# One in-order queue for loads and stores, and tiles of twice the size, in a streaming gated-GELU kernel

## The chip, the cores and the metric

The kernel runs on one core of one Trainium2 chip. The metric is the time of the program on the device in microseconds (us), as the median of several runs. The profiled span is about 1.9 us shorter than that time (474.1 against 476.0 us before). Most differences here are below 2%, so each run was timed beside the kernel before, on the same chip in the same rounds.

## The reference

The input is `x`, 32 x 512 x 2048 float32 (134.2 MB). The last axis is split in two halves; the output is 32 x 512 x 1024 float32 (67.1 MB):

```python
x1, x2 = x[..., :1024], x[..., 1024:]
gelu_x1 = 0.5 * x1 * (1 + erf(x1 / np.sqrt(2)))
return (gelu_x1 * x2).astype(np.float32)
```

Every byte is read or written once, 201.3 MB in all. There is no reuse.

## The kernel before

Rows are laid out so that each of the 128 partitions holds R consecutive rows of a tile. With R = 4 a load moves 4 MB, 32 KB contiguous per partition, and a store 2 MB, 16 KB per partition. There are 32 tiles. Loads are issued by SP (`nc.sync`), stores by ACT (`nc.scalar`): two queues.

```python
    R = 4
    x_t = x_flat.rearrange("(n p r) d -> n p r d", p=P, r=R)
    o_t = out_flat.rearrange("(n p r) d -> n p r d", p=P, r=R)
    n_tiles = x_t.shape[0]

    xpool = ctx.enter_context(tc.tile_pool(name="xpool", bufs=4))
    opool = ctx.enter_context(tc.tile_pool(name="opool", bufs=4))

    for i in range(n_tiles):
        x_tile = xpool.tile([P, R, dim], x.dtype)
        nc.sync.dma_start(out=x_tile, in_=x_t[i])

        o_tile = opool.tile([P, R, half], out.dtype)
        for r in range(R):
            nc.scalar.activation(out=x_tile[:, r, :half], in_=x_tile[:, r, :half],
                                 func=mybir.ActivationFunctionType.Gelu)
            nc.vector.tensor_mul(out=o_tile[:, r, :], in0=x_tile[:, r, :half],
                                 in1=x_tile[:, r, half:])
        nc.scalar.dma_start(out=o_t[i], in_=o_tile)
    # ... (launch code cut)
```

## Time and profile before

| | before |
|---|---|
| time, median | 476.0 us (475.94 to 476.09) |
| profiled span | 474.1 us |
| DMA queues' packet time | 98.9% of 16 engines' span |
| DVE, ACT busy | 31%, 27% |

From the page of the kernel before, parts 1 to 3. In part 2 the span is cut into 40 slices; a DMA digit of 9 means that the 16 DMA engines were at least 90% busy in that slice. In part 3, q1 carries SP's loads and q10 ACT's stores.

```profile
DVE 148.2 (31%) x128; ACT 125.9 (27%) x129; POOL 0.2 (0%) x4
...
DMA  8999999999999999999999999999999999999995
...
q1 hardware_dynamic: 4608, 134.22, 65.8%
q10 hardware_dynamic: 4608, 67.11, 33.1%
```

So the DMA engines bound the kernel, and only the first and the last slice have room. The next view cuts the end of the span into short windows. The columns are window, its length, busy time of DVE, ACT and POOL, the TensorE clock, then the DMA share and GB/s; the first line is one tile's period from the middle.

```profile
60.00:74.54 14.54, 4.63 (x4) 3.90 (x4) 0.00 (x0) 1.00 1.00 433
...
460.00:462.00 2.00, 0.55 (x1) 1.64 (x2) 0.00 (x0) 1.00 1.07 459
462.00:464.00 2.00, 2.00 (x3) 2.00 (x3) 0.00 (x0) 1.00 0.71 303
464.00:466.00 2.00, 2.00 (x2) 0.25 (x1) 0.00 (x0) 1.00 0.04 16
466.00:467.00 1.00, 0.08 (x1) 0.00 (x0) 0.00 (x0) 1.00 0.27 115
467.00:470.00 3.00, 0.00 (x0) 0.00 (x0) 0.00 (x0) 1.00 0.95 396
470.00:472.00 2.00, 0.00 (x0) 0.00 (x0) 0.00 (x0) 1.00 0.93 393
```

A share of 1.00 in the middle: nothing to win there but cheaper packets. (A share can pass 1, by 0.07 in these lines, because a packet's whole time is booked where it starts.) Between 462 and 467 us there is a hole: all earlier transfers have drained, and the last store waits for the last tile's arithmetic.

The trace also has a record for every DMA packet: start, duration, bytes and queue, but not the engine. Two things can be worked out from these records. First, a 32 KB load packet takes 1213 ns and a 16 KB store packet 611 ns at the median (27 bytes per ns and engine). Second, every load and store here ends with 16 4-byte packets (1024 for the 64 of them), by continuity one on each engine; the time from the first to the last of these 16 tells how far the engines stand apart. I call it the *spread*. (Which packets belong to one engine can be told by continuity: on an engine, a packet starts about 4 ns before the record of the one before it ends.)

### The profile page before, as it was taken

How to read it: one execution, taken by the hardware profiler on the slowest of the kernel's cores; microseconds unless marked ns; L12 is line 12 of the kernel's file. 1: busy time of each engine (PE TensorE's matmuls, PEld its weight loads, DVE VectorE, ACT ScalarE, POOL GpSimd, SP SyncE). 2: the span in 40 equal slices, each digit the busy share in tenths (PEclk: the TensorE clock that was granted, in tenths of full speed). 3: DMA queues.
4: the chain of work that ended last, by engine and by line, in shares of the span. 5: the costliest groups of instructions: out<-in, count | busy, mean ns of one | idle time of the engine just before them, and what ended most of it. 6: DMA issues, size and time to landing. Idle time of an engine off the chain costs nothing.

```text
span 474.1 us, 509 instructions
## 1 busy us (share of the span) xinstructions
DVE 148.2 (31%) x128; ACT 125.9 (27%) x129; POOL 0.2 (0%) x4
## 2 busy tenths in 40 slices
DVE  0333321333312333123332133331233321333213
ACT  1423331133321333213333123332133331233311
POOL 0000000000000000000000000000000000000000
DMA  8999999999999999999999999999999999999995
GB/s 354 406 456 408 455 417 445 419 444 420 442 420 443 421 440 427 435 433 430 438 427 452 412 451 413 452 413 452 413 451 420 445 419 444 421 440 423 440 423 225
DMA packets 9220, 201.36 MB, mean 425 GB/s; under 512 B 1024, under 2 KB 1024, under 8 KB 1024
## 3 DMA queue, kind: packets, MB, share of 16 engines
q1 hardware_dynamic: 4608, 134.22, 65.8%
q10 hardware_dynamic: 4608, 67.11, 33.1%
q14 instruction: 4, 0.03, 0.0%
HBM read 134.22 MB, written 67.11 MB: 425 GB/s over the span
## 4 chain that ended last, share of the span: by engine, by line
another core or an unknown queue 48%; DVE 27%; DMA 13%; ACT 7%; issue 2%; ACTq 2%; DVEq 0%
DVE o_tile L45 27%; DMA x_tile<-in_x_dram 13%; ACT x_tile L40 7%; ACTq L50 2%; DVEq L76 0%; ACTq L40 0%
## 5 line engine op out<-in xcount | busy, mean ns | idle before, releaser
L45 DVE TENSOR_TENSOR o_tile<-x_tile 128x1024 f32<-128x1024 f32 x128 | 148.2, 1219 | 317.9 <-ACT x_tile L40 317.9
L40 ACT ACTIVATE x_tile<-x_tile 128x1024 f32<-128x1024 f32 x128 | 124.7, 1044 | 337.6 <-DMA x_tile<-in_x_dram 337.6
L40 ACT ACT_TABLE_LOAD x1 | 1.3, 1283 | 0.7 <-PEq L65 0.7
L65 POOL MEMSET const-uint8-127<- 128x1 uint8 x1 | 0.1, 102 | 0.0
L65 POOL MEMSET const-bfloat16-1.0<- 128x1 bf16 x1 | 0.1, 101 | 0.0
L65 POOL MEMSET const-float32-0.0<- 128x1 f32 x1 | 0.1, 99 | 0.2 <-issue 0.2
L65 POOL MEMSET const-float32-1.0<- 128x1 f32 x1 | 0.1, 99 | 0.0
## 6 DMA issues: line engine op xcount, KB each, us to landing
x_tile<-in_x_dram SPq DMA_DIRECT2D x32, 4096.0 KB, 52.3
out_dram<-o_tile ACTq DMA_DIRECT2D x32, 2048.0 KB, 23.4
```

Of the source, the lines that this page charges most:

```text
L40: nc.scalar.activation(out=x_tile[:, r, :half], in_=x_tile[:, r, :half], func=mybir.ActivationFunctionType.Gelu,)
L45: nc.vector.tensor_mul(out=o_tile[:, r, :], in0=x_tile[:, r, :half], in1=x_tile[:, r, half:],)
L50: nc.scalar.dma_start(out=o_t[i], in_=o_tile)
L65: nc = _bacc.Bacc("TRN2", target_bir_lowering=False, num_devices=1)
```

## The change

The intent: one queue in a fixed order instead of two that compete; half as many, twice as large transfers; and a shorter tail, because the last tile's store is cut in four. The diff's core (launch code and renamings cut):

```diff
-    R = 4
+    R = 8
...
-    xpool = ctx.enter_context(tc.tile_pool(name="xpool", bufs=4))
-    opool = ctx.enter_context(tc.tile_pool(name="opool", bufs=4))
+    xpool = ctx.enter_context(tc.tile_pool(name="xpool", bufs=2))
+    opool = ctx.enter_context(tc.tile_pool(name="opool", bufs=2))
+    def load(i):
+        x_tile = xpool.tile([P, R, dim], x.dtype, name="x_tile")
+        nc.sync.dma_start(out=x_tile, in_=x_t[i])
+        return x_tile
+
+    ahead = [load(0), load(1)]
     for i in range(n_tiles):
-        x_tile = xpool.tile([P, R, dim], x.dtype)
-        nc.sync.dma_start(out=x_tile, in_=x_t[i])
+        x_tile = ahead.pop(0)
+        o_tile = opool.tile([P, R, half], out.dtype, name="o_tile")
...
+        pieces = 1 if i < n_tiles - 1 else 4
+        step = R // pieces
+        for k in range(pieces):
+            for r in range(k * step, (k + 1) * step):
+                ...   # Gelu and multiply of row r, as before
+            rows = slice(k * step, (k + 1) * step)
+            nc.sync.dma_start(out=o_t[i][:, rows, :], in_=o_tile[:, rows, :])
+        if i + 2 < n_tiles:
+            ahead.append(load(i + 2))
-        nc.scalar.dma_start(out=o_t[i], in_=o_tile)
```

The queue of SP becomes L0 L1 S0 L2 S1 L3 ... L15 S14 and four pieces of S15.

More of the change, by code (lines that the diff above doesn't have):

```diff
@@ L7 @@
 from concourse._compat import with_exitstack
+GELU = mybir.ActivationFunctionType.Gelu
 @with_exitstack
@@ L29 @@
     n_tiles = x_t.shape[0]
-    xpool = ctx.enter_context(tc.tile_pool(name="xpool", bufs=4))
-    opool = ctx.enter_context(tc.tile_pool(name="opool", bufs=4))
-    for i in range(n_tiles):
-        x_tile = xpool.tile([P, R, dim], x.dtype)
-        nc.sync.dma_start(out=x_tile, in_=x_t[i])
-        o_tile = opool.tile([P, R, half], out.dtype)
-        for r in range(R):
-            nc.scalar.activation(
-                out=x_tile[:, r, :half],
-                in_=x_tile[:, r, :half],
-                func=mybir.ActivationFunctionType.Gelu,
-            )
-            nc.vector.tensor_mul(
-                out=o_tile[:, r, :],
-                in0=x_tile[:, r, :half],
-                in1=x_tile[:, r, half:],
-            )
-        nc.scalar.dma_start(out=o_t[i], in_=o_tile)
+    xpool = ctx.enter_context(tc.tile_pool(name="xpool", bufs=2))
[5 more added lines that the diff above has]
+    ahead = [load(0), load(1)]
+    for i in range(n_tiles):
+        x_tile = ahead.pop(0)
[4 more added lines that the diff above has]
+            for r in range(k * step, (k + 1) * step):
+                nc.scalar.activation(
+                    out=x_tile[:, r, :half], in_=x_tile[:, r, :half], func=GELU
+                )
+                nc.vector.tensor_mul(
+                    out=o_tile[:, r, :],
+                    in0=x_tile[:, r, :half],
+                    in1=x_tile[:, r, half:],
+                )
+            rows = slice(k * step, (k + 1) * step)
+            nc.sync.dma_start(out=o_t[i][:, rows, :], in_=o_tile[:, rows, :])
+        if i + 2 < n_tiles:
+            ahead.append(load(i + 2))
 _INS = ['x']
```

## The prediction

> **What bounds the kernel now.** The 16 DMA engines. The page's DMA row is 9 tenths or more in every slice but the first and last; the two queues take 65.8% + 33.1% = 98.9% of 16 engines' span. ACT is busy 27%, DVE 31%. Cut into stretches of 14.54 us (one tile's period) from 60 to 452 us, each shows DMA share 1.00 to 1.01 and 432 to 433 GB/s. In the packet records a 32 KB load packet takes 1213 ns at the median, a 16 KB store packet 611 ns, whether loads run alone (5 to 18 us), both interleave, or stores run alone (460 to 463 us). With 256 of each per engine that is 310.5 + 156.4 = 466.9 us of a span of 474.1. The other 7 us are the start (about 1.5), the drain after the last store (about 2) and a hole at the end: the DMA share is 0.71 in 462 to 464 us, 0.04 in 464 to 466, 0.27 in 466 to 467. Store 30 has drained, and the last tile's Gelu and multiply (460.4 to 466.1) must end before its store starts. The hole is 0.58 + 1.92 + 0.73 = 3.2 us.
>
> **What the change does.**
> 1. Stores move from ACT's queue to SP's. [...] the load queue alone already has share 1.0. Worth 0. ACT loses 32 issues of 0.36 us, off the critical path.
> 2. In-order waits: the queue becomes L0 L1 S0 L2 S1 L3 ... Store i and load i+2 both wait for tile i's multiply, so neither holds up the other. Compute of an 8-row tile is an estimated 1.1 + 8 x 1.22 = 11 us after its load; the queue then still holds about 18 us of work (store i-1 9.7, load i+1 19.4), in the first round 8 us. The engines never run dry.
> 3. Packets double. 1213 - 2 x 611 = -9 ns: about 9 ns are fixed per packet. Halving 512 packets per engine saves an estimated 2.3 us; the 8 KB packets of the last stores give 0.2 back. Worth 2 us, or 1 if 64 KB rows are cut in two.
> 4. The tail. Store 14 stands behind load 15 and lasts 9.7 us while the last tile computes; its first quarter is ready after 3.6 us, its last after 11. So the 3.2 us hole goes.
>
> **Sum.** 474.1 - 3.2 - 2.0 = 468.9 us of span; times are 1.9 us above the span: **471.0 us**, 8 in 10 between **469.0 and 473.5**, about 1% faster. Chances: faster by over 2% 0.02 (466.5 us is less than data plus start and drain), within 2% 0.94, slower by over 2% 0.04.
>
> **Right if:** the DMA row stays at 9 until 2 us before the end, share 1.00 in every period of about 29 us, no hole after the last load; load packets near 2417 ns, store packets near 1213; SP waits for DVE only.
>
> **Wrong if:** one queue has a bubble at a store's end. [...] load-to-load boundaries in the first 20 us show no loss, but no store-to-load boundary within one queue is in this trace. At 0.5 us each they would cost 8 us and eat the gain. Or 64 KB packets behave differently, or one engine lags.

## The result, and the profile after

| | before | after |
|---|---|---|
| time, median of 4 runs | 475.97 us | 475.73 us |
| lowest to highest | 475.91 to 476.09 | 474.72 to 476.17 |
| profiled span | 474.1 us | 472.7 us (of the 474.72 us run) |

The ratio is 0.9993, 95% interval 0.9978 to 1.0007. Ratios are the mean time of one kernel's fast runs over that of the other's in the same rounds, so not quite the ratio of the medians. The predicted 471.0 us (469.0 to 473.5) was too low: nearly nothing was gained. The runs after differ by 1.5 us, those before by 0.2 us.

From the page after, parts 1 to 3:

```profile
DVE 146.8 (31%) x128; ACT 124.2 (26%) x129; POOL 0.2 (0%) x4
...
DMA  8999999999999999999999999999999999999996
...
q1 hardware_dynamic: 5040, 201.33, 99.0%
```

SP's waits after (who waited for whom, us in total, times, longest):

```profile
SPq L58 <- DVE o_tile L52: 447.1, 19, 31.3
SPq L86 <- DMA out_dram<-o_tile: 8.7, 1, 8.7
```

And windows after, one 8-row period from the middle, then the end:

```profile
70.00:99.08 29.08, 9.17 (x8) 7.68 (x8) 0.00 (x0) 1.00 1.00 433
...
456.00:460.00 4.00, 4.00 (x4) 4.00 (x5) 0.00 (x0) 1.00 0.89 381
460.00:464.00 4.00, 2.60 (x3) 0.03 (x1) 0.00 (x0) 1.00 0.99 418
464.00:467.00 3.00, 0.00 (x0) 0.00 (x0) 0.00 (x0) 1.00 1.01 429
467.00:468.00 1.00, 0.00 (x0) 0.00 (x0) 0.00 (x0) 1.00 0.99 418
468.00:470.00 2.00, 0.00 (x0) 0.00 (x0) 0.00 (x0) 1.00 0.39 164
470.00:472.00 2.00, 0.00 (x0) 0.00 (x0) 0.00 (x0) 1.00 0.10 41
```

Most of the prediction is visible: SP waits for DVE alone until its final wait, the DMA share is 1.00 in the middle, and the hole before the last store is gone. But the span does not end at 468 us plus the drain. In 468 to 472 us the share is 0.39 and then 0.10: most of the 16 engines have finished, and a few still work. The packet records say the same. Sorted, the ends of the 16 engines' last packets are (us from the span's start):

```
before: 471.89 471.89 471.89 471.89 471.91 471.92 471.92 471.94 471.96 471.97 471.98 471.98 471.99 472.02 472.02 472.83
after:  467.93 468.02 468.04 468.05 468.05 468.20 468.45 468.57 468.75 468.83 468.90 469.98 470.59 470.67 471.06 471.41
```

(These are ends of 4-byte packets, one for each engine, put together by continuity. The last 16 such packets of the trace would not do after the change: the slowest engines are more than one piece, 2.5 us, behind, so four of the 16 would be ends of the piece before.) The earliest engines finish where the prediction wanted all of them. Where does the difference come from? The spread at the end of successive DMAs shows it (start of the 16 packets: spread, both in us):

```
before, loads : 21.9: 0.44   138.6: 0.49   167.7: 1.18   313.2: 1.18   458.6: 1.24
after, L0..L3 : L0 21.7: 0.64   L1 42.1: 0.67   S0 51.7: 0.67   L2 71.1: 0.73   S1 80.8: 0.73   L3 100.1: 0.89   S2 109.8: 0.89
after, later  : L4 129.1: 1.15  S3 138.8: 1.15  L5 158.2: 1.39  S4 167.8: 1.39  L6 187.2: 1.70  ...  L15 448.4: 3.48
```

After the change the spread grows from load to load and never from a load's end to the next store's end. It is the last packet of a load, the one in front of a store, that is stretched. A 64 KB load packet normally takes 2418 ns; the 16 last packets of L1 (at 39 us, in front of S0) took 3240 to 3868 ns, 1.07 us more in the mean. At later boundaries some engines lose 0 to 0.6 us and others nothing. No engine of the core computes at 39 us (tile 0 is done at 32.9, tile 1 starts at 43.1 us), so it is not traffic of ACT or DVE. Before, load packets after the first 4 us lose only 0.58 us per engine in all, 0.51 of it when the first store joins the loads at about 21 us; one engine lags by another 0.7 us from 153 us on, and then almost nothing changes. I call it *stretch*.

**Theory A.** In one in-order queue every load-to-store boundary is a turn of the engine; turns stretch the last load packet, differently on each engine, nothing brings the engines together again, and the program ends with its slowest engine. **Rival B.** The 64 KB packets or the large tiles do it.

### The profile page after: what moved, and what is told of

Its sections match the earlier page's. It is cut to its first block, busy times and chain, and to the rows that moved or that the text cites. A ratio compares the mean times of both kernels' runs of the same rounds, so it can differ in the third digit from the quotient of the medians.

```text
span 472.7 us, 394 instructions
## 1 busy us (share of the span) xinstructions
DVE 146.8 (31%) x128; ACT 124.2 (26%) x129; POOL 0.2 (0%) x4
## 4 chain that ended last, share of the span: by engine, by line
DMA 79%; DVE 15%; ACT 2%; SPq 1%; issue 0%; DVEq 0%; ACTq 0%
DMA x_tile<-in_x_dram 79%; DVE o_tile L52 15%; ACT x_tile L49 2%; SPq L58 1%; DVEq L86 0%; SPq L37 0%; ACTq L49 0%
## 5 line engine op out<-in xcount | busy, mean ns | idle before, releaser
L49 ACT ACTIVATE x_tile<-x_tile 128x1024 f32<-128x1024 f32 x128 | 122.9, 1042 | 335.1 <-DMA x_tile<-in_x_dram 335.1
```

## The experiments

### Only the queue: e1_one_queue_r4

```diff
-        nc.scalar.dma_start(out=o_t[i], in_=o_tile)
+        nc.sync.dma_start(out=o_t[i], in_=o_tile)
```
(on the kernel before)

> The kernel before with one edit: stores issued from SP's queue, 4 rows and undivided last store kept. Theory A (the changed kernel loses its gain at load-to-store boundaries inside one queue: the last load packet of some engines is stretched there, each engine by a different sum, and the program ends with the slowest engine): 31 boundaries instead of 15, so load packets (nominal 1213 ns) are stretched near every boundary, excess at least 3 us per engine in the mean, time 476 to 480 us, not below the kernel before. Theory B (64 KB packets or the large tiles are what stretches and spreads): no stretch here, the hole before the last store shrinks, time about 474.5 us.

Measured: 477.2 us, ratio 1.0027 (1.0015 to 1.0040), slower than before. The spread grew from 0.67 us at the first load to 3.46 us at 110 us and then stayed there to the last load. The load stretch was 0.74 us at the start and 1.2 us later. So B falls: 32 KB packets and small tiles do it too, and moving the queue alone costs time. But A as stated also missed: I expected at least 3 us of stretch with twice as many boundaries, and it all but stopped by itself once the engines stood 3.5 us apart (0.2 us per engine after 115 us).

### Only the tail: e2_last_tile_pieces

```diff
+            if i == n_tiles - 1:
+                nc.sync.dma_start(out=o_t[i][:, r, :], in_=o_tile[:, r, :])
-        nc.scalar.dma_start(out=o_t[i], in_=o_tile)
+        if i < n_tiles - 1:
+            nc.scalar.dma_start(out=o_t[i], in_=o_tile)
```
(on the kernel before)

> The kernel before with one edit: the last tile stored row by row (4 stores of 512 KB, from SP, which has no loads left). Both theories: the 3.2 us hole at 464 to 467 us nearly closes and nothing else changes: time 473.2 us, 2.8 us below before (range 472.6 to 474.0). If it gains less than 1.5 us, the hole was not worth what I took for it, and that is where the prediction failed.

Measured: 473.44 us, ratio 0.9944 (0.9931 to 0.9958): 2.5 us gained. Windows of this kernel, to be read against 462 to 467 us of the kernel before:

```profile
462.00:464.00 2.00, 2.00 (x3) 2.00 (x3) 0.00 (x0) 1.00 0.90 350
464.00:466.00 2.00, 2.00 (x2) 0.30 (x1) 0.00 (x0) 1.00 0.99 408
466.00:467.00 1.00, 0.12 (x1) 0.00 (x0) 0.00 (x0) 1.00 1.05 426
```

The hole was real and worth about what the prediction said. That term is not what failed.

### The change without the single queue: e3_two_queues_r8

```diff
-            nc.sync.dma_start(out=o_t[i][:, rows, :], in_=o_tile[:, rows, :])
+            q = nc.scalar if i < n_tiles - 1 else nc.sync
+            q.dma_start(out=o_t[i][:, rows, :], in_=o_tile[:, rows, :])
```
(on the changed kernel)

> The changed kernel with one edit: all stores but the last tile's back on ACT's queue; 8 rows, two buffers, 4 pieces kept. Theory A: no stretched packets beyond the first store (excess under 1.5 us per engine, as in before), load packets 2418 ns, hole at the end about 1.5 us: time 472.4 us (471.5 to 473.5), clearly faster than the changed kernel's 475.7. Theory B: stretched 64 KB packets remain, time 475 us or more.

Measured: 472.63 us, ratio 0.9929 (0.9917 to 0.9942). Against the changed kernel's 475.73 us that is 3.1 us for the queue alone, with all other parts of the change kept (not the same rounds, but the kernel before ran beside both, at 475.97 and 475.96 us, and the two intervals lie far apart). Windows at the end of this kernel:

```profile
464.00:467.00 3.00, 0.00 (x0) 0.00 (x0) 0.00 (x0) 1.00 1.01 426
467.00:468.00 1.00, 0.00 (x0) 0.00 (x0) 0.00 (x0) 1.00 1.02 434
468.00:470.00 2.00, 0.00 (x0) 0.00 (x0) 0.00 (x0) 1.00 0.36 152
470.00:470.60 0.60, 0.00 (x0) 0.00 (x0) 0.00 (x0) 1.00 0.00 0
```

The engines end between 468.28 and 469.28 us, so the 2 us with few engines at work are gone. The stretch is 1.43 us per engine when the first store joins the loads (34 to 39 us; more than I expected) and 0.05 us in all the rest of the run; the first 8 KB store packets of the last tile lose another 0.6 us at 458 us. The mean end of the engines, 468.86 us, is only 0.2 us earlier than the changed kernel's 469.09. What the second queue saves in these two traces is mostly the difference between the slowest engine and the mean: 0.42 us instead of 2.31.

### The last store whole: e4_last_tile_whole

```diff
-        pieces = 1 if i < n_tiles - 1 else 4
+        pieces = 1
```
(on the changed kernel)

> The changed kernel with one edit: the last tile stored in one piece. Both theories: the last load lands at about 452.5 us, compute ends 11 us later, first packets of the last store at 465, 9.8 us of store and 1.3 of drain: span about 476, time about 478 us (476.8 to 479), some 2 us slower than the changed kernel; by theory A all 16 engines start that last store together, so their ends agree to 0.3 us, where in the changed kernel they spread over 3.5 us.

Measured: 477.29 us, ratio 1.0028 (1.0015 to 1.0040). The engines reached the end of the last load and of the store before it with a spread of 5.18 us, started the last store together after it had been issued at 464.4 us, and ended within 0.15 us of each other. Two lessons. The pieces are worth 1.6 us in one queue. And the DMAs up to that point are the same as in the changed kernel, whose spread was 3.48 us there: how far the engines drift differs from run to run. This goes with the 1.5 us by which the changed kernel's runs differ.

### Engines set apart on purpose: e5_engines_staggered

The fading of the stretch in e1 suggested what a turn costs: contention among engines that turn at the same moment (A1), rather than a fixed price (A2). To test this, five small loads of unequal size are to set the engines apart. The trace of this run has 45 data packets of 12 KB for them and 45 closing 4-byte packets, 3 + 6 + 9 + 12 + 15. It has no engine numbers, so no run here shows which engines they ran on. The recorded cost is an estimate: at the measured 27 bytes per ns a packet of 12 KB takes 0.46 us, so 45 of them 1.3 us per engine in the mean, and five on one engine 2.3.

```diff
+    spool = ctx.enter_context(tc.tile_pool(name="spool", bufs=1))
+    stairs = spool.tile([45, 3072], x.dtype, name="stairs")
+    x_wide = x_flat.rearrange("(a b) d -> a (b d)", b=2)
+    at = 0
+    for n in (3, 6, 9, 12, 15):
+        nc.scalar.dma_start(out=stairs[at : at + n, :], in_=x_wide[:n, :3072])
+        at += n
```
(on the changed kernel, before the first loads)

> The changed kernel with one addition: at the start five small unused loads of 3, 6, 9, 12 and 15 partitions (12 KB each) from ACT's queue[...]. It adds work (1.3 us per engine in the mean, 2.3 at most). Theory A1 (the stretch at a load-to-store boundary is contention among engines that turn at the same time): the excess at the first boundary falls from 1.07 us per engine to under 0.5, and the total beyond the start from 2.2 us to under 1.2; time 473.5 to 475.5 us despite the added work. Theory A2 (each engine pays a fixed price for its first turn): the first boundary stays at 1.0 to 1.3 us, time 476.5 us or more.

Measured: 479.24 us, ratio 1.0070 (1.0058 to 1.0083). The time missed A1's range, and by its number alone it would fit A2. The trace says otherwise. The small loads disturbed the first 30 us far more than I had allowed for: load packets lost 4.2 us per engine between 4 and 30 us, and L0 landed at 30.9 instead of 22.7 us. But the spread at L0's end was 4.39 us instead of 0.64, and at the first load-to-store boundary (L1's end at 46 us, spread 3.38) not one load packet was stretched by over 40 ns, where the changed kernel lost 1.07 us per engine. After 60 us load packets lost 0.03 us in all. Engines set apart in this way did not stretch each other's packets. That the run was slow for its own start, and because it ends with a spread of 3.9 us, fits the trace but was not tested alone.

### More boundaries: e6_one_queue_r2 and e9_one_queue_r2_deep

```diff
-    R = 4
+    R = 2
```
(on e1's kernel)

> The kernel of the first run (all in one queue, last store whole) with 2 rows per tile: 63 boundaries instead of 31. Theory A1: once the engines stand some 3 to 4 us apart they no longer turn together and stretching stops, so the spread at the end is 2.5 to 4.5 us as with 31 and with 15 boundaries, and mean excess beyond the start stays under 2 us. Theory A2' (a price per boundary): excess and spread double or more. Smaller packets (611 and 309 ns) add 4 us by themselves, so time 479 to 481 us by A1, 482 or more by A2'.

Measured: 522.66 us, ratio 1.0983 (1.0968 to 1.0998), far beyond A1's range. Packets lost 35 us per engine, but 25 of it were on store packets: in every second tile 26 to 39 of the 128 8 KB packets took about 606 ns instead of 309. The DMAs were issued only a few us ahead (6.6 us from issue to landing of a store whose data take 2.5), and the spread fell back to 2 us every second tile, which looks like fast engines running out of work. So it could not be read, and I ran it with more work in the queue:

```diff
-    R = 8
+    R = 2
-    xpool = ctx.enter_context(tc.tile_pool(name="xpool", bufs=2))
-    opool = ctx.enter_context(tc.tile_pool(name="opool", bufs=2))
+    xpool = ctx.enter_context(tc.tile_pool(name="xpool", bufs=6))
+    opool = ctx.enter_context(tc.tile_pool(name="opool", bufs=6))
-    ahead = [load(0), load(1)]
+    ahead = [load(k) for k in range(6)]
-        pieces = 1 if i < n_tiles - 1 else 4
+        pieces = 1
-        if i + 2 < n_tiles:
-            ahead.append(load(i + 2))
+        if i + 6 < n_tiles:
+            ahead.append(load(i + 6))
```
(on the changed kernel)

> All in one queue with 2 rows per tile again, but six loads ahead instead of two (six buffers), so that every DMA is issued some 30 us before its turn and no engine can run out of work; in the earlier 2-row run it came only about 4 us ahead, so that run could not be read. 63 load-to-store boundaries. Theory A1: stretching fades once the engines stand apart, spread at the end 2.5 to 4.5 us, excess beyond the start under 2.5 us per engine; smaller packets add 4 us: time 479 to 481.5 us. A price per boundary: about 4 times the 2.2 us of the changed kernel's 15 boundaries, 9 us, so 485 us or more. If the 8 KB store packets again take 606 ns instead of 309 in some tiles, running out of work was not their cause.

Measured: 478.18 us, ratio 1.0047 (1.0031 to 1.0064), 0.8 us below A1's range and 7 below the rival's. With 59 boundaries (not the 63 expected: the last five stores follow a store) the stretch after the first 4 us was 1.4 us per engine, less than with 15 (2.21); 1.1 us of it came before 46 us, and the spread stayed between 2.3 and 3.6 us from 47 us on. Store packets took 309 ns. There is no price per boundary, and what made e6 slow went away with a deeper queue. Why some packets of a nearly empty queue took double was not looked into.

### Engines brought together again: e8_one_queue_r4_realigned

```diff
+        if i == 17:
+            nc.vector.memset(o_15[:, 0, :1], 0.0)
+            nc.vector.tensor_copy(out=x_tile[:, 0, :1], in_=o_15[:, 0, :1])
         nc.sync.dma_start(out=x_tile, in_=x_t[i])
...
+        if i == 15:
+            o_15 = o_tile
```
(on e1's kernel; the copy can run only when the store of tile 15 has landed, and load 17 only after the copy)

> The kernel of the first run (all in one queue, 4 rows per tile), with the queue made to drain once in the middle: loads from tile 17 on wait until the store of tile 15 has landed, so that the 16 engines start together again at about 250 us. In the first run they stood 3.46 us apart by then and no load packet was stretched after 191 us. Theory A1 (contention among engines that turn from load to store together): the spread falls below 1 us at the pause, the next load-to-store boundary (about 25 us after it) stretches load packets again, 0.2 us per engine or more in the mean, and the spread grows again. Rival (the stretching is something of the first 200 us of a run that wears off): no stretching after the pause. The time rises by the pause itself (2 to 4 us) and is not the point.

Measured: 484.25 us, ratio 1.0169 (1.0139 to 1.0198); the pause cost more than the 2 to 4 us that I had expected. From the packet records, the spread at the ends of DMAs and the stretch near them:

```
226.3: 3.84   240.8: 3.84   245.7: 3.84     no load packet stretched from 213 to 255 us
pause; 257.1: 0.70   267.1: 0.40
277.3: 0.65 (first load-to-store boundary after it: 23 load packets stretched, 0.50 us per engine)
306.5: 0.87   335.6: 1.09   364.7: 1.88   379.4: 2.47   437.5: 2.81
```

The stretch had stopped; with the engines together again it came back at once, and the spread grew again. It is not a matter of the first part of a run. This fits A1, with a limit that is told under "Why the prediction was wrong". (That a restart of the queue brings stretch of its own was not separated; but the spread still grew 180 us after the pause.)

### Is there more in the tail: e7_two_queues_r8_8pieces

```diff
-        pieces = 1 if i < n_tiles - 1 else 4
+        pieces = 1 if i < n_tiles - 1 else 8
```
(on e3's kernel)

> The changed kernel with stores on ACT's queue, and the last tile in 8 pieces of one row instead of 4 of two. In the version with 4 pieces the engines had no gap left at the end, so nothing should come of it: time 472.0 to 473.0 us. Were the end still waiting for the first piece, it would gain about 1 us (471.5).

Measured: 472.34 us, ratio 0.9928 (0.9914 to 0.9941), as the kernel with 4 pieces. Both beat the kernels before and after by 3.1 to 3.6 us and are the best versions found: 8 rows, two queues, last tile in pieces.

## Why the prediction was wrong

The terms, per engine, from the packet records of the two profiled runs. "Packet time" is the sum of normal durations less the overlap of neighbours; "lag" is the slowest engine's end less the mean end.

| term | before | after | change | predicted |
|---|---|---|---|---|
| packet time | 466.9 - 2.1 = 464.8 | 465.0 - 1.1 = 463.9 | -0.9 | -2.0 |
| hole before the last store | 3.2 | 0 | -3.2 | -3.2 |
| stretch of load packets after 4 us | 0.58 | 2.21 | +1.6 | 0 |
| lag of the slowest engine | 0.83 | 2.31 | +1.5 | 0 |
| sum | | | -1.0 | -5.2 |
| span | 474.1 | 472.7 | -1.4 | -5.2 |

The sum meets the measured change of the span within 0.4 us. The run that was profiled after was the fastest of its four; the median lies another 1.0 us higher, which no trace covers.

Point by point:

- **The DMA engines bound it, and double buffering suffices: right.** SP waited for DVE only, and the share was 1.00 in the middle.
- **The hole goes, 3.2 us: right.** e2 gained 2.5 us from that alone.
- **Packets worth 2 us: right in sign, mis-sized.** Load packets took 2418 ns (2417 predicted), stores 1213; a 64 KB row went as one packet (2048 of them). But each record overlaps the next by about 4 ns, so the price of a packet is nearer 5 ns than the 9 that I took from 1213 - 2 x 611. The term is about 0.9 us.
- **"Stores move from ACT's queue to SP's ... Worth 0": this step failed.** The prediction drew it from the load queue's share of 1.0 when running alone (1.00 at 434 GB/s from 4 to 8 us). Nothing in the runs speaks against that share, but it does not say that a turn from load to store inside one queue is free; that was my estimate, and no trace had shown it. It cost 3.1 us between e3 and the changed kernel, and 1.2 us (477.2 against 475.96) at 4 rows. In the profiled runs before and after, the table has it as stretched load packets (+1.6 us) and a slowest engine further behind the mean (+1.5 us).
- **The stated risk pointed at the wrong boundary.** I named a bubble at a store's end. The store packets, those in front of a load included, lost 0.08 us per engine in the whole run after the change, and no engine showed a gap behind a store; it is mostly the load packet in front of a store that is stretched. "One engine lags" was named too, without a size. It is the larger part of what e3 wins back.

What is shown: one queue costs the time (e1, e3); not packet or tile size (e1, e9); not the number of boundaries (e9); with the engines set apart from the start the stretch did not come (e5), and with the engines brought together it came back (e8).

Which engines pay, the experiments did not ask, but their packet records show it, and A1's wording fits the first boundary only. There, in the changed kernel, all 16 lost 0.8 to 1.5 us. Of what was lost at the later boundaries, the eight engines that reached a boundary last bore 84% (91% in e4, 75% in e1). At L13's end (390 us) the eleven engines that turned first, within 1.0 us, lost at most 0.04 us each, and the five that came 1.6 to 2.9 us behind them 0.13 to 0.57. In e4, at 420 us and a spread of 4.6 us, the first eleven lost at most 0.03 us, the last five 0.50 to 0.94. And in e1, at 51 us, an engine 2.6 us behind lost 1.05 us on its last load packet but one, before its own turn. So the loss falls mostly on engines that still load when others have gone over to stores, and drives them further behind. A large spread alone does not end it, and some boundaries cost nothing (L14 and L15 of the changed kernel); what decides that is open.

In the kernel before, both queues always have work and the spread stays as it is over hundreds of us (1.18 us from 167.7 to 400.4 us, 1.24 after the last load and after the last store but one; e3 has 1.05 us there). The trace shows loads and stores alternating packet by packet: 128 load and 128 store packets in one period of 14.54 us of the steady part, at least 32 of each in every 4 us, and in all 4792 pairs of neighbouring data packets between 60 and 452 us that continuity puts on one engine with no second candidate, a load follows a store or a store a load. So an engine turns all the time, and nearly all of the stretch of load packets is seen when the first store joins (0.51 of 0.58 us per engine). (Here the spread is the same at a load's end and at the end of the store beside it: 0.49 and 0.48 us at 36.8 us, 1.24 at both at 458.6 us.) Which resource the engines contend for is open: the trace does not name it, and no run separated the memories.

## What to carry to other kernels

Here, with the DMA engines full, a single in-order queue that switches between loads and stores let the 16 engines drift 3.5 us apart, and the program waited for the slowest. In such a kernel, try a queue each for loads and stores, so that both always have work (3.1 us gained here). Average share (99.0%) and packet medians (2418 and 1213 ns) did not show this: look at when each of the 16 engines ends. Judge the parts of a change one at a time: here two good parts (pieces and larger packets, 3.3 us together in e3) were hidden by one bad part (the queue, 3.1 us) almost exactly.
